# A hybrid attention, scan and latent-attention trunk on one core: five scratch arrays kept by token tile, the scan part projected first, one rotated query projection, and the last softmax denominators on 64 rows

## The chip, the core and the metric

The kernel runs on one core of a Trainium2 chip. A core has five engines that run their own instruction streams side by side: TensorE (PE in the profile; PEld is its weight load), VectorE (DVE), ScalarE (ACT), GpSimd (POOL) and SyncE (SP), which here issues nearly all DMA transfers. TensorE writes to PSUM, eight banks of 128 rows by 512 floats; all other operands lie in SBUF, 128 rows wide; large arrays lie in DRAM and move by DMA on 16 DMA engines. Engines wait for each other by semaphores.

The metric is the time of one execution on the device in microseconds (us), compared as the median of several runs.

## The reference, cut to what matters

Two layers run on 1024 latent tokens and 128 context tokens (T = 1152, nine tiles of 128), width 1024. Layer 0 runs windowed attention (8 heads) beside a bidirectional state-space scan (16 heads of 64, chunks of 128 tokens, both directions); layer 1 is latent attention with 16 heads, whose queries have 64 plain and 32 rotated features:

```python
y = y_f + flip(y_b) + d_skip[:, None] * xs
...
a_out = attn.reshape(b, L, A_WIDTH) * jax.nn.silu(g)
s_out = rms_norm(y.reshape(b, L, SSD_INNER) * jax.nn.silu(z), gnorm_w)
return jnp.concatenate([a_out, s_out], axis=-1) @ w_out
...
xr = jnp.concatenate([rot(x[..., :half]), rot(x[..., half:])], axis=-1)
return x * cos.reshape(shape) + xr * sin.reshape(shape)
...
out = dense_attention(q[:, :, :, None, :], k, v, MLA_SCALE)
return (out.reshape(b, L, MLA_WIDTH) * jax.nn.silu(g)) @ w_out
```

`rot(u)` swaps the two halves of a group of 16 features and negates one. `dense_attention` is a softmax: exponentials of scores, divided by their sum (the denominator). Each layer ends with `x + gate * out`, then comes the next norm. All is float32.

## The kernel before

**Number format.** Most products are done in three matmuls (`mm3`, lines 255 to 258): each operand is split by `split` (245 to 253) into a rounded high part (ScalarE, 249 or 252) and a low part (VectorE, 250 or 253), and high by high, high by low and low by high are summed in one PSUM bank.

**Stages in order.** (1) Modulation and the normalised, transposed input (lines 421 to 456). (2) Keys, values, queries and the gate z of the scan; z goes to `z_d`, feature block by feature block (line 699). (3) `convs` with `attention0` and `chunk_states` woven in (720 to 919): ten blocks of 128 features are projected, convolved, and the eight x blocks written both ways, tokens on rows (`xs_d`, line 900) and features on rows (`xT_d`, 898 and 899). The weights of a block are fetched two blocks ahead by `slab` (line 302). (4) `gates0` (947) multiplies the attention output by its gate and writes `a_d` (959), while `scan_out` starts with two tiles. (5) A loop over the nine token tiles (1158 to 1168): `scan_out` of one tile runs beside `project_out` of the tile before. (6) The latents of layer 1 from `h1_d` (1211 to 1243). (7) `gates1`, the gates of layer 1. (8) Eight pairs of heads (1624 to 1654). (9) The output projection of layer 1, the residual and the last norm, tile by tile (1667 to 1694).

**Scan loop.** `scan_out` loads B and C, `xs_d`, the tile of `xT_d` (990) and `z_d` (993), the states `H_d` and four rows-to-all-partitions copies of the cumulated decays `cum_d` (1004, 512 KB each). It forms the score product `Gp` (984) in a bank of the PSUM ring "pre", the decays with GpSimd (1013) and ScalarE (1015), and the y products (1022). `project_out` loads the attention part (`project_operands`, 1087), and for each half of the output multiplies the attention part (12 matmuls, "plain", PSUM ring "pre") and the scan part (24 matmuls, "scaled", ring "mm"). ScalarE copies plain to SBUF (1105), VectorE adds scaled times a norm factor to it (1106), GpSimd applies gate and residual. A square over the tile (1114) and `norm_T` (1057) follow: transposes, two VectorE operations per half into a buffer of the ring "rt" (two buffers, shared with line 1104), and a write to `h1_d`.

**Pairs.** For each pair `pair_main` does the scores (1470 to 1472), exponentials (ScalarE, 1477), sums (GpSimd, 1506) and values (1491). The operands of the next pair are made in between by `spread`: `quad_weights` and `quad_rope` once in four heads, `operands` (with `rotated`) once a pair, and `head_max`, which finds each query's maximum (1449, VectorE reductions recorded at 209) and sends it to row 96 of the query operand (1441), which the last score product (1472) needs. `quad_rope` does two projections of 128 rotated features per column chunk, one with the weights in order and one with their halves swapped (`swapped`, 1333), and multiplies them by the cosine and sine tables (1367). `gather` divides by the denominators: a one-row product (1522), the row through DRAM (`rd1_d`) to 64 rows and back, a reciprocal on 64 rows, and a copy to all rows (1545). Pair 7 runs its three column chunks in the order 0, 2, 1, and the output projection of tile 0 needs the first of them.

**Order of work.** `Steps` (193) runs deferred parts a given number of score groups later; `pinned` keeps an instruction at its place in the program. For the rest the order of each engine's instructions is set when the program is built, by a planner with its own estimates of durations. Engines then run in that order: an instruction that waits holds all behind it on its engine. Rings of buffers work the same way: a new tile waits for the last reader of the buffer that it takes over.

The scratch arrays touched here, as they were:

```python
a_d = scratch("a_d", [4, 128, T])
xT_d = scratch("xT_d", [KT, 128, T])
z_d = scratch("z_d", [KT, 128, T])
h1_d = scratch("h1_d", [KT, 128, T])
o1_d = scratch("o1_d", [KT, 128, T])
```

A read of one token tile from these takes 512 bytes (128 floats) for each feature and block; a write of a feature block takes long rows. The profile drops digits in the names of DRAM arrays: `h_d` is `h1_d`, `o_d` is `o_d` or `o1_d`, `rd_d` is `rd_d` or `rd1_d`. SBUF tiles lie in four arenas, arenaR, S, G and F.

## Time and profile before

| what | value |
|---|---|
| median of 3 runs | 1848.65 us |
| lowest and highest | 1847.19 and 1849.92 us |
| the profiled execution, its own time | 1851.17 us |
| its span, first to last instruction | 1849.4 us |
| mean granted TensorE clock | 0.952 of full speed |
| DMA | 219.67 MB in 229567 packets, 119 GB/s over the span |
| the hardware queue's share of 16 DMA engines | 39.8% |

How to read the lines further down: a page line gives busy us, share of the span and, behind x, the number of instructions. A line of groups has source line, engine, operation, out<-in, shape and count, then busy us and the mean ns of one, then the engine's idle time before them with what ended it. A waits line names who waited for whom: us in total, times, longest. A timeline line has start, duration, engine, line, operation, and in brackets the idle time just before with what ended it. SPq is SyncE issuing a DMA; its duration is that of the issue, not of the transfer. A line of one source line has count, then min/median/max in ns and the first and last start. Matmuls follow each other closer than their durations, so the pace is read from their starts.

### The profile page before, as it was taken

How to read it: one execution, taken by the hardware profiler on the slowest of the kernel's cores; microseconds unless marked ns; L12 is line 12 of the kernel's file. 1: busy time of each engine (PE TensorE's matmuls, PEld its weight loads, DVE VectorE, ACT ScalarE, POOL GpSimd, SP SyncE). 2: the span in 40 equal slices, each digit the busy share in tenths (PEclk: the TensorE clock that was granted, in tenths of full speed). 3: DMA queues.
4: the chain of work that ended last, by engine and by line, in shares of the span. 5: the costliest groups of instructions: out<-in, count | busy, mean ns of one | idle time of the engine just before them, and what ended most of it. 6: DMA issues, size and time to landing. Idle time of an engine off the chain costs nothing.

```text
span 1849.4 us, 26784 instructions
## 1 busy us (share of the span) xinstructions
PE 1679.6 (91%) x8881; PEld 1293.5 (70%) x8881; DVE 1047.0 (57%) x1977; ACT 866.1 (47%) x1941; POOL 731.0 (40%) x728
## 2 busy tenths in 40 slices
PE   6899998998999778698789999999999999999898
PEld 2799998886876667566569898655665665654486
DVE  3755545556464567678785534665665665565243
ACT  4632222556565456566653422435545634545321
POOL 2510000024333333554634011455665574565432
PEclk8999999999999889899899999999999999999999
DMA  6513323344444889657562533020121121114342
GB/s 224 160 51 113 100 73 110 115 133 137 116 141 140 232 255 279 202 173 222 178 200 86 165 112 101 10 62 23 46 68 32 44 61 45 31 34 122 109 154 91
DMA packets 229567, 219.67 MB, mean 119 GB/s; under 512 B 37283, under 2 KB 194545, under 8 KB 229429
## 3 DMA queue, kind: packets, MB, share of 16 engines
q1 hardware_dynamic: 229284, 217.84, 39.8%
q8 instruction: 70, 1.15, 0.3%
q14 instruction: 69, 0.56, 0.1%
q0 software_dynamic: 144, 0.13, 0.0%
HBM read 156.65 MB, written 56.44 MB: 115 GB/s over the span
## 4 chain that ended last, share of the span: by engine, by line
PE 65%; DMA 13%; ACT 5%; DVE 5%; issue 3%; POOL 2%; SPq 2%; POOLq 0%; DVEq 0%; ACTq 0%
PE acc L256 11%; PE acc L258 10%; PE acc L257 10%; PE acco L1491 6%; PE pp L1449 3%; PE sc L1470 3%; PE sc L1472 3%; PE sc L1471 3%; DMA arenaG<-cum_d 2%; DMA arenaF<-rd_d 2%; DMA rd_d<-arenaF 2%; ACT arenaG L1015 2%; DMA arenaF<-xT_d 1%; PE st L811 1%; DVE arenaR L250 1%
## 5 line engine op out<-in xcount | busy, mean ns | idle before, releaser
L1506 POOL TENSOR_TENSOR arenaG<-arenaG 128x512 f32<-128x512 f32 x256 | 334.2, 1324 | 223.7 <-ACT arenaG L1477 196.6
L256 PE MATMUL acc<-arenaR 128*128 128x384 f32 (+4 forms) x1128 | 392.2, 349 | 31.5 <-ACT arenaR L249 11.7
L257 PE MATMUL acc<-arenaR 128*128 128x384 f32 (+3 forms) x1056 | 362.2, 343 | 0.1
L258 PE MATMUL acc<-arenaR 128*128 128x384 f32 (+4 forms) x1032 | 350.6, 341 | 0.1
L1477 ACT ACTIVATE arenaG<-sc 128x512 f32<-128x512 f32 (+1 forms) x304 | 174.7, 580 | 219.1 <-PE sc L1472 210.8
L256 PEld LDWEIGHTS acc<-arenaR 128*128 128x128 f32 x1128 | 218.2, 194 | 66.4 <-ACT arenaR L249 13.3
L209 DVE TENSOR_REDUCE arenaF<-pp 128x1 f32<-128x384 f32 (+1 forms) x400 | 199.2, 539 | 110.2 <-PE pp L1449 108.7
L257 PEld LDWEIGHTS acc<-arenaR 128*128 128x128 f32 x1056 | 203.9, 193 | 12.6 <-issue 2.8
L258 PEld LDWEIGHTS acc<-arenaR 128*128 128x128 f32 x1032 | 199.1, 193 | 12.7 <-issue 1.5
L250 DVE TENSOR_TENSOR arenaR<-arenaF,arenaR 128x512 fp32r<-128x512 f32 (+2 forms) x144 | 128.4, 904 | 89.9 <-ACT arenaR L249 88.0
L249 ACT CAST arenaR<-arenaF 128x512 fp32r<-128x512 f32 (+3 forms) x160 | 101.0, 648 | 135.0 <-DMA arenaF<-in_ab_w_in_dram 24.2
L1491 PE MATMUL acco<-arenaG 128*64 128x512 f32 (+1 forms) x608 | 150.4, 610 | 0.0
L752 POOL TENSOR_TENSOR arenaG<-arenaS,arenaG 128x512 fp32r<-128x512 f32 x26 | 43.7, 1679 | 155.8 <-PE acco L756 66.7
L1015 ACT ACTIVATE arenaG<-arenaG,arenaF 128x128 f32<-128x128 f32 x288 | 89.8, 390 | 26.6 <-POOL arenaG L1013 26.1
L1449 PE MATMUL pp<-arenaR 96*128 96x384 f32 (+1 forms) x300 | 91.9, 362 | 11.0 <-DVE arenaF L209 10.5
L1470 PE MATMUL sc<-arenaR 96*128 96x512 f32 (+1 forms) x228 | 94.4, 414 | 4.8 <-ACT arenaG L1477 4.5
L1449 PEld LDWEIGHTS pp<-arenaR 96*128 96x128 f32 x300 | 54.7, 190 | 54.2 <-DVE arenaF L209 23.5
L1472 PE MATMUL sc<-arenaR 97*128 97x512 f32 (+1 forms) x228 | 89.0, 394 | 1.3 <-DMA arenaR<-arenaF 1.3
L1471 PE MATMUL sc<-arenaR 96*128 96x512 f32 (+1 forms) x228 | 89.3, 392 | 0.0
L1491 PEld LDWEIGHTS acco<-arenaG 128*64 128x64 f32 x608 | 36.9, 140 | 70.1 <-issue 67.1
L573 POOL TENSOR_TENSOR arenaF<-arenaF 128x256 f32<-128x256 f32 (+1 forms) x27 | 18.4, 684 | 160.1 <-DVE arenaF L571 94.6
L1013 POOL TENSOR_SCALAR_AFFINE_SELECT arenaG<-arenaG 128x512 f32<-128x512 f32 x72 | 61.7, 869 | 50.0 <-ACT arenaF L1009 28.1
(330 smaller groups left out, 3473.6 us busy)
## 6 DMA issues: line engine op xcount, KB each, us to landing
arenaF<-in_ada_w_dram SPq DMA_DIRECT2D x96, 256.0 KB
arenaG<-cum_d SPq DMA_DIRECT2D x36, 512.0 KB
arenaF<-in_ab_w_in_dram SPq DMA_DIRECT2D x51, 256.0 KB
z_d<-arenaF SPq DMA_DIRECT2D x24, 192.0 KB
xs_d<-arenaF SPq DMA_DIRECT2D x8, 576.0 KB
arenaF<-z_d SPq DMA_DIRECT2D x9, 512.0 KB
arenaF<-xT_d SPq DMA_DIRECT2D x9, 512.0 KB
arenaF<-xs_d SPq DMA_DIRECT2D x9, 512.0 KB
```

The costliest lines, as they stand in the source:

```text
L209: f()
L250: lo_eng.tensor_tensor(lo, src, hi.bitcast(F32), ALU.subtract)
L256: pe.matmul(out, ah, bh, start=first, stop=False)
L257: pe.matmul(out, ah, bl, start=False, stop=False)
L258: pe.matmul(out, al, bh, start=False, stop=last)
L1449: pe.matmul(pp[:, 0:w], AQ[s][0:96, t * 128:(t + 1) * 128], AK[s][0:96, k0:k0 + w], start=True, stop=True)
L1470: pe.matmul(sc[:, 0:n], AK[s][0:96, ks], BQ[s][:, qs], start=True, stop=False)
L1471: pe.matmul(sc[:, 0:n], BK[s][:, ks], AQ[s][0:96, qs], start=False, stop=False)
L1472: pe.matmul(sc[:, 0:n], AK[s][:, ks], AQ[s][:, qs], start=False, stop=True)
L1477: act.activation(pf, sc[:, 0:n], AF.Exp, scale=SCALE_M)
L1491: put = lambda: pe.matmul(acc[0][a * 64:(a + 1) * 64], V[:, a], pfs[a], start=(i < 2 and k < 2), stop=(last and k >= len(todo) - 2))
L1506: pool.tensor_tensor(totals[a], first[a] if i == 1 else totals[a], pfs[a], ALU.add)
```

## The change

Five scratch arrays are kept by token tile, so that a tile is read in one piece per partition; the writes of z, xT, a and the attention output go to several tiles at once through `by_tile`. `project_out` multiplies the scan part first, ScalarE scales it while the attention part is multiplied, and VectorE adds. `norm_T` transposes all eight blocks first and writes its result over its input. In layer 1 the 128 rotated features of a quad are ordered so that the two halves of each group lie 64 rows apart; the sine part then comes from the same projection, by two products of 64 rows each with exchanged row halves, and the second projection and `swapped` go. The tables, the split of the weights, and the copies in `operand_set` and `rotated` follow that order, in more and smaller pieces. For pair 7 the denominators are formed on 64 rows by a column block of ones, and divided in place (`gather_last`).

```diff
+    def by_tile(dst, k, t0, src):
+
+        n = src.shape[1] // 128
+        dma.dma_start(dst[t0:t0 + n, :, k].rearrange("t p n -> p t n"), src.rearrange("p (t n) -> p t n", n=128))
...
-    a_d = scratch("a_d", [4, 128, T])
+    a_d = scratch("a_d", [NT, 128, 4, 128])
-    xT_d = scratch("xT_d", [KT, 128, T])
-    z_d = scratch("z_d", [KT, 128, T])
+    xT_d = scratch("xT_d", [NT, 128, KT, 128])
+    z_d = scratch("z_d", [NT, 128, KT, 128])
-    h1_d = scratch("h1_d", [KT, 128, T])
+    h1_d = scratch("h1_d", [NT, 128, KT, 128])
-    o1_d = scratch("o1_d", [KT, 128, T])
+    o1_d = scratch("o1_d", [NT, 128, KT, 128])
...
-                        dma.dma_start(xT_d[fb][:, 0:NL], th[:, 0:NL])
-                        dma.dma_start(xT_d[fb][:, NL:T], th[:, NL + 2:W])
+                        by_tile(xT_d, fb, 0, th[:, 0:NL])
+                        by_tile(xT_d, fb, NLT, th[:, NL + 2:W])
...
-        dma.dma_start(y, xT_d[:, :, tok].rearrange("k p n -> p k n"))
+        dma.dma_start(y, xT_d[c])
...
+        pts = [psum("tr", "pt") for _ in range(2)]
         for q in range(2):
-            pt = psum("tr", "pt")
             for j in range(4):
-                pe.transpose(pt[:, j * 128:(j + 1) * 128], xh[:, (q * 4 + j) * 128:(q * 4 + j + 1) * 128], ident)
-            full = p.tile([128, 4, 128], F32, tag="rt", name="nf", bufs=2)
+                pe.transpose(pts[q][:, j * 128:(j + 1) * 128], xh[:, (q * 4 + j) * 128:(q * 4 + j + 1) * 128], ident)
+        for q in range(2):
+            full = xh[:, q * 512:(q + 1) * 512].rearrange("p (k n) -> p k n", k=4)
...
-            for k in range(4):
-                mm3(plain, at[:, 0, k], at[:, 1, k], *wos[k, q], k == 0, k == 3)
             for k in range(8):
                 mm3(scaled, sT[:, 0, k], sT[:, 1, k], *wos[k + 4, q], k == 0, k == 7)
             tmp = p.tile([128, 512], F32, tag="rt", name="rt", bufs=2)
-            act.copy(tmp, plain)
-            dve.scalar_tensor_tensor(tmp, scaled, r, tmp, ALU.mult, ALU.add)
+            act.activation(tmp, scaled, AF.Identity, scale=r)
+            for k in range(4):
+                mm3(plain, at[:, 0, k], at[:, 1, k], *wos[k, q], k == 0, k == 3)
+            dve.tensor_tensor(tmp, plain, tmp, ALU.add)
...
-        dma.dma_start(AK[i][64:96].bitcast(F32), kp_d[0])
-        dma.dma_start(BK[i][64:96].bitcast(F32), kp_d[1])
-    ones = p7.tile([128, 1], F32, name="ones")
+        for u in range(2):
+            for s in range(2):
+                to, at = slice(64 + s * 16 + u * 8, 72 + s * 16 + u * 8), slice(u * 16 + s * 8, u * 16 + s * 8 + 8)
+                dma.dma_start(AK[i][to].bitcast(F32), kp_d[0, at])
+                dma.dma_start(BK[i][to].bitcast(F32), kp_d[1, at])
+    ones = p7.tile([128, 64], F32, name="ones")
...
-            for a, b, w, at in ((0, 64, 64, 0), (64, 96, 32, 256)):
-                o = slice(at, at + 4 * w)
...
+            split(qh[:, k, 0:256].rearrange("p (h d) -> p h d", h=4), ql[:, k, 0:256].rearrange("p (h d) -> p h d", h=4), raws[k][:, :, 0:64], scale)
             for s in range(2):
-                dve.tensor_copy(dst[:, :, :, s], src[:, :, :, 1 - s].bitcast(F32))
+                for u in range(2):
...
+                    split(part(qh), part(ql), raws[k][:, :, at:at + 8], scale)
...
-            for i, t in enumerate(ts):
-                after(1, dve.tensor_tensor, t, uq_proj(qh, ql, 256 + 128 * i, cols), tab[:, i], ALU.mult)
-                yield
+            acc = uq_proj(qh, ql, 256, cols)
+            after(1, dve.tensor_tensor, ts[0], acc, tab[:, 0], ALU.mult)
+            for s in range(2):
+                at, to = slice(s * 64, (s + 1) * 64), slice((1 - s) * 64, (2 - s) * 64)
+                after(1, dve.tensor_tensor, ts[1][to], acc[at], tab[at, 1], ALU.mult)
+            yield
...
+            i, h = (4 * Q + 2 * pr + a) % NSET, 2 * pr + a
+            for s in range(2):
+                to, r = slice(64 + s * 16, 80 + s * 16), slice(s * 64 + h * 16, s * 64 + h * 16 + 16)
+                for dst, src in ((AQ, quads[Q][1][0]), (BQ, quads[Q][1][1])):
+                    dma.dma_start(dst[i][to].bitcast(F32), src[r].bitcast(F32))
...
+    def gather_last(j, op, q0, n, totals):
+
+        qs = slice(q0, q0 + n)
+        gt = p7.tile([128, n], F32, tag=f"gt{n}", name="gt1")
+        rb = p7.tile([128, n], F32, tag=f"rb{n}", name="rb1")
+        dma.dma_start(gt, g1_d[j, :, qs])
+
+        def sums():
+            den = spare("den")
+            for a in range(2):
+                pe.matmul(den[a * 64:(a + 1) * 64, 0:n], ones, totals[a], start=True, stop=True)
+            dve.tensor_tensor(gt, op[:, qs], gt, ALU.mult)
+            after(1, divided, den)
+
+        def divided(den):
+            dve.reciprocal(rb, den[:, 0:n])
+            dve.tensor_tensor(gt, gt, rb, ALU.mult)
+            by_tile(o1_d, j, q0 // 128, gt)
+        steps.behind(1, sums)
...
+        if j == 7:
+            return gather_last(j, op, q0, n, totals)
...
-            make, n_make = [operands(pair + 1)], 22
+            make, n_make = [operands(pair + 1)], 19
```

The other reads and writes of the five arrays (`z_d`, `a_d`, `h1_d`, `o1_d`) change as those of `xT_d` do.

More of the change, by code (lines that the diff above doesn't have):

```diff
@@ L958, in gates0 @@
             dve.tensor_tensor(th, th, ot, ALU.mult)
-            dma.dma_start(a_d[b, :, cols], th)
+            by_tile(a_d, b, c * 3, th)
             if b == 3:
@@ L1521, in sums @@
             for a in range(2):
-                pe.matmul(den[a * 64:a * 64 + 1, 0:n], ones, totals[a], start=True, stop=True)
+                pe.matmul(den[a * 64:a * 64 + 1, 0:n], ones[:, 0:1], totals[a], start=True, stop=True)
             after(1, store, den)
```

37 lines of the change are left out of this document (16 added, 21 removed).

## The prediction

> **What bounds the kernel now.** I read the page first, then busy time by stage, then the waits of TensorE and the timelines around the longest ones.
>
> ```profile
> span 1849.4 us, 26784 instructions
> PE 1679.6 (91%) x8881; PEld 1293.5 (70%) x8881; DVE 1047.0 (57%) x1977; ACT 866.1 (47%) x1941; POOL 731.0 (40%) x728
> ```
>
> TensorE (PE) is busy 91% of the span; 169.8 us are left. The stage view (stretch, its length, busy us per engine, granted clock, DMA share, GB/s) says where they lie. Rows in order: convolutions with attention; attention gates; the loop of scan and output projection; the latent layer's gates; the eight head pairs.
>
> ```profile
> 318.00:640.00 322.00, 294.18 (x1590) 233.93 (x1590) 179.68 (x288) 187.83 (x380) 98.81 (x103) 0.94 0.49 141
> 640.00:741.00 101.00, 81.27 (x466) 68.99 (x465) 67.20 (x103) 56.15 (x128) 38.90 (x39) 0.89 0.94 270
> 741.00:969.00 228.00, 184.72 (x1070) 144.22 (x1070) 173.29 (x200) 138.60 (x342) 118.21 (x118) 0.90 0.65 194
> 1005.00:1150.00 145.00, 142.15 (x822) 133.73 (x821) 60.62 (x137) 49.86 (x121) 18.26 (x30) 1.00 0.41 119
> 1150.00:1736.00 586.00, 553.02 (x2454) 336.92 (x2454) 337.18 (x695) 286.32 (x621) 349.83 (x273) 0.97 0.18 51
> ```
>
> Two kinds of stage. In the gates and the pairs TensorE is busy 98% and 94% of the time (142.15 of 145, 553.02 of 586), no other engine over 60%: a matmul taken out there is time taken out. In the scan loop TensorE lacks 43.3 us (228 - 184.72) and VectorE is busy 76%; there waits decide. The longest:
>
> ```profile
> PE Gp L984 <- ACT arenaF L1105: 26.2, 4, 13.2
> ```
>
> ```profile
> 768.78 0.59 ACT L1105 COPY arenaF<-acca 128x512 f32<-128x512 f32 x1 [5.89 <-DMA h_d<-arenaF]
> ```
>
> Four times, 26.2 us in all, the score product Gp of a later tile waits for a PSUM bank that ScalarE's copy at L1105 must empty. In the worst (13.2 us) ScalarE itself stood idle 5.89 us, until a write into h1_d had left the buffer that the copy needs: the ring "rt" of two, shared by L1104 and L1063.
>
> **Part by part.**
>
> *norm_T in place.* The h1_d writes now leave from xn, so L1104 no longer shares "rt" with them. Of the 13.2 us wait the 5.89 go; what was late before them (ScalarE's exponentials and a square, until 762.9) stays. The new wait is the next tile's square into xn, which has one buffer; it comes a tile later (228 us for nine tiles, 25 each) and the late write was over by 768.78, so I cost it at nothing, and at 5.9 a tile if that cover were gone. **-5.9**.
>
> *Reading xT_d, z_d, a_d, h1_d in rows of 4 KB or 2 KB instead of 512-byte pieces.* First bandwidth, in two stretches of 4 us when the queue was full, the first with 512-byte pieces of z_d, the second with 4 KB rows:
>
> ```profile
> DMA packets 2086, 1.06 MB, mean 266 GB/s; under 512 B 38, under 2 KB 2082, under 8 KB 2086
> ...
> q1 hardware_dynamic: 2086, 1.06, 91.5%
> ```
>
> ```profile
> DMA packets 327, 1.22 MB, mean 304 GB/s; under 512 B 30, under 2 KB 30, under 8 KB 327
> ...
> q1 hardware_dynamic: 327, 1.22, 99.7%
> ```
>
> 266/0.915 = 291 GB/s against 304/0.997 = 305 at full share: 5%, or 0.1 us on a transfer of 512 KB. The Trainium skill ("DMA: Bandwidth & Descriptors", Specifications) names 512 B as the smallest transfer for line rate; by it this edit would give nothing, and the sum would be 7.5 us smaller. On bandwidth the two stretches nearly agree with it. What the pieces do cost stands on SyncE:
>
> ```profile
> 870.25 0.37 SPq L993 DMA_DIRECT2D arenaF<-z_d  x1
> 870.72 4.50 SPq L1004 DMA_DIRECT2D arenaG<-cum_d  x1
> ```
>
> An issue takes 0.37 us, but the one behind xT_d and z_d (1024 pieces each, 2 x 512 KB / 512 B) takes 4.50. In the chain of work that ended last (start, us, what) this transfer, and two reads of xT_d, stand at full length:
>
> ```profile
> 838.80 8.30 DMA arenaF<-xT_d
> ```
>
> ```profile
> 870.72 9.45 DMA arenaG<-cum_d
> ```
>
> ```profile
> 898.67 10.37 DMA arenaF<-xT_d
> ```
>
> ```profile
> 807.35 5.97 DMA arenaG<-cum_d
> ```
>
> The last is the same 512 KB in 4 KB rows without the hold-up: 5.97. I take 4.1 for the held issue (4.50 - 0.37), and for the two reads half of their excess (8.30 + 10.37 - 2 x 5.97 = 6.7, so 3.4), since part of it is other traffic. **-7.5**, bounds 0 and -10.8. In the other stages I cost the reads at nothing: 640 to 741 runs the DMA at a share of 0.94 either way, and the output loop feeds a busy TensorE.
>
> *Writing in 512-byte pieces.* z_d, a_d and o1_d are written 384 or 512 pieces at a time over long stages; xT_d goes from 256 to 1152 pieces a block, eight times, right after a write of the same kind:
>
> ```profile
> L900 SPq DMA_DIRECT2D xs_d<-arenaF x8: 370/383/546, 391.0 to 637.9; - x8
> ```
>
> xs_d is 1152 pieces (9 tiles x 128 rows) and issues in 0.38 us. Two in a row are what held 870.72 up for 4.1 us: bounds 0 and 8 x 4.1 = 33 us of SyncE. Hidden, it lies under the weights being fetched two blocks ahead, a block being some 32 us (322 / 10): I take 0.
>
> *Scan part first in project_out.* The same 72 matmuls; now ScalarE scales while the 12 plain ones run, and VectorE's addition empties the bank that Gp waits for. Instructions and engines stay even (one ScalarE, one VectorE operation for one of each). ScalarE gets a lead of 12 x 0.23 us = 2.7 (the spacing of these matmuls at full pace, rows 1740.78 and 1741.01 below), but VectorE now stands behind it: 0, bounds +-2.7 for each of the other three waits.
>
> *One rotated projection.* uq_proj is 6 matmuls of 384 columns; one of two goes, for 3 column chunks and 4 quads: 72.
>
> ```profile
> 1256.37 0.34 PE L256 MATMUL acc<-arenaR 128*128 128x384 f32 x1
> 1256.54 0.33 PE L257 MATMUL acc<-arenaR 128*128 128x384 f32 x1
> 1256.71 0.34 PE L258 MATMUL acc<-arenaR,arenaS 128*128 128x384 f32 x1
> 1256.89 0.34 PE L256 MATMUL acc<-arenaR 128*128 128x384 f32 x1
> ```
>
> They overlap, so the spacing counts: 0.52/3 = 0.173 us, and 72 x 0.173 = **-12.5** (54 in the pairs, 18 in the gates). What is added:
>
> ```profile
> L250 DVE TENSOR_TENSOR arenaR<-acc,arenaR 64x384 fp32r<-64x384 f32 x36 | 19.8, 551 | 11.5 <-ACT arenaR L249 10.7
> ```
>
> ```profile
> L253 DVE SCALAR_TENSOR_TENSOR arenaS<-arenaF,vecs,arenaR 128x128 fp32r<-128x128 f32 x6 | 2.3, 379 | 5.9 <-ACT arenaR L252 5.9
> ```
>
> ```profile
> L1333 DVE CAST arenaR<-arenaR x8: 209/216/220, 1075.7 to 1383.9; 128x128 fp32r<-128x128 f32 x8
> L1333 DVE CAST arenaS<-arenaS x8: 208/216/219, 1075.9 to 1384.7; 128x128 fp32r<-128x128 f32 x8
> ```
>
> ```profile
> L1236 DVE TENSOR_TENSOR arenaF<-acc,arenaF x8: 178/180/181, 987.2 to 1023.0; 128x32 f32<-128x32 f32 x8
> ```
>
> VectorE: 12 more half-height products at 0.55 (+6.6), 8 splits of 128 columns become 32 of 32 columns at about 0.18 (+2.7), 16 swaps at 0.216 go (-3.5): +5.8 us, over stages where it is idle 42% or more of the time. ScalarE gains 24 small splits, 4.3 us at the same 0.18. Both lie beside matmuls; uncovered they would cost at most 5.8. SyncE:
>
> ```profile
> L1404 SPq DMA_DIRECT2D arenaR<-arenaF x24: 512/552/870, 1112.5 to 1596.9; - x24
> ```
>
> rotated issues 8 instead of 4 per pair: +32 x 0.55 = 17.6 us; operand_set +24, by this row 13 at most. Queued behind them is the row of maxima (L1441) that a score product needs; rotated goes out at a pair's start, the maxima some ten steps later. If all were exposed it would be 4 x 0.55 = 2.2 us in each of 7 pairs, 15.4. Of VectorE and SyncE together I let 1.5 us through, as both have long idle stretches there (DMA share 0.18). Net **-11.0**, bounds -12.5 and +8.7 (5.8 and 15.4 in full).
>
> *Last denominators.* Pair 7 no longer sends its sums through DRAM. Now (the chain, then TensorE):
>
> ```profile
> 1709.02 3.83 DMA rd_d<-arenaF
> ```
>
> ```profile
> 1730.75 4.70 DMA arenaF<-o_d
> ```
>
> ```profile
> 1736.56 0.79 PE L256 MATMUL acc<-arenaR 128*128 128x512 f32 x1 [6.63 <-ACT arenaR L249]
> 1737.15 0.63 PE L257 MATMUL acc<-arenaR 128*128 128x512 f32 x1
> 1737.58 0.63 PE L256 MATMUL acc<-arenaR 128*128 128x512 f32 x1
> ```
>
> ```profile
> 1740.78 0.39 PE L257 MATMUL acc<-arenaR 128*128 128x512 f32 x1
> 1741.01 0.40 PE L258 MATMUL acc<-arenaR 128*128 128x512 f32 x1
> ```
>
> From the sums (stored at 1709.0) to the first operand's load (1730.75) are 21.7 us; then TensorE has stood 6.63 us, and starts at half pace: 0.43 us apart against 0.23; over the 3.4 us to about 1740 that loses 3.4 x 0.20/0.43 = 1.6. The new path is a reciprocal and a product:
>
> ```profile
> L511 DVE RECIPROCAL arenaS<-arenaS x1: 1953/1953/1953, 110.5 to 110.5; 128x288 f32<-128x288 f32 x1
> ```
>
> 1953/288 = 6.8 ns a column, 3.5 us for 512 as an estimate, plus 0.7 for the product (0.55 for 384 columns, L250 above). The load can then start near 1709 + 4 + 4 (a write like the one at 1709.02) = 1717, 14 us earlier, and TensorE goes from the last scores straight into the output: -6.6 - 1.6 = **-8.2**. What is late next is the residual input, needed 24 matmuls (5.5 us) later. Bounds -8.2 and 0.
>
> **Sum.** -5.9 - 7.5 - 11.0 - 8.2 = -32.6. The profiled execution took 1851.17 us (span 1849.4 and 1.8 around it): 1818.6. The median of the three runs, 1848.65, lies 2.5 lower, so I forecast 1816 (-1.8%).
>
> **The rivals.** (1) *The scan loop gains nothing.* For it: VectorE at 76%, bandwidth alike in both forms, and all instructions are put in order anew at build time, so that waits can come back elsewhere. Against it: ScalarE's 5.89 and SyncE's 4.50 have named causes that the diff removes. Left are -11.0 - 8.2: 1851.2 - 19.2 - 2.5 = 1829.5. The rule of the Trainium skill quoted above ("DMA: Bandwidth & Descriptors", Specifications) speaks for this rival. (2) *The loop's waits all fall together.* Idle 43.3 us, and a granted clock of 0.90: if two thirds of the idle go (-29 instead of -13.4), 1851.2 - 29 - 19.2 - 2.5 = 1800.5. (3) *SyncE is held up in the convolutions*, on the other side: xT_d's 1152 pieces behind xs_d's 1152 hold the next weights by 4.1 us in 8 blocks, and TensorE waits each time: +33. With rival 1's loop that is 1829.5 + 33 = 1862.5, with my own 1849. It decides only where weights arrive less than 4 us early; TensorE's 294 of 322 us leave 28 idle, so some such place exists, eight do not. (4) *The pairs give nothing back*: the matmuls go, but ScalarE's exponentials or VectorE's maxima set the pace, -11.0 becomes -2: 1825. Against it: neither is over 60% busy there.
>
> **How the numbers follow.** Forecast 0.55, rivals 0.20, 0.13, 0.06, 0.06. Measurement of this kernel tells about 0.2% (3.7 us) from no change; only rival 3, and the far end of rivals 1 and 4, get to 1845 or above: faster 0.90, same 0.04, slower 0.06. From 1798 (just past rival 2) to 1841 (rival 1 with the pairs giving nothing, 1829.5 + 11) leaves out rival 3 and the ends of the others, some two in ten.
>
> **What would show it.** Right: no wait of the first evacuation in project_out on a write of h1_d; cum_d issues all under 1 us; 72 fewer matmuls of 384 columns and a stretch of pairs some 11 us shorter; no gap of 6.63 us before the first output product. Wrong: SyncE issues of 3 us or more between 360 and 640, a score product waiting for maxima rows by more than the present few us, or a scan loop still near 228 us.

## The result and the profile after

The changed kernel took 1840.59 us in the median of 20 runs (1831.03 to 1850.28), the kernel before 1851.78 in 20 runs on the same chip (1844.57 to 1859.22). The ratio is 0.9935, with a 95% interval of 0.9915 to 0.9955: 12 us faster, with 8 to 16 possible. Forecast were 33. The profiled execution of the changed kernel took 1847.63 us, near the slow end of its runs.

The page after (span; busy time by engine), and the stage view over the stretches that answer to those of before, each shifted to where its stage now lies. Columns: stretch, length, busy us of PE, PEld, DVE, ACT, POOL with counts, granted clock, DMA share, GB/s.

```profile
span 1845.5 us, 26718 instructions
...
PE 1692.1 (92%) x8809; PEld 1291.7 (70%) x8809; DVE 1062.7 (58%) x1998; ACT 868.6 (47%) x1959; POOL 729.8 (40%) x727
```

```profile
640.00:741.00 101.00, 83.33 (x473) 69.32 (x473) 67.61 (x105) 55.54 (x129) 37.70 (x37) 0.89 0.88 268
741.00:960.00 219.00, 188.49 (x1084) 146.89 (x1085) 176.04 (x203) 143.02 (x346) 122.71 (x121) 0.94 0.61 205
995.00:1135.00 140.00, 138.08 (x796) 129.10 (x794) 60.88 (x139) 51.07 (x131) 18.87 (x30) 1.00 0.42 118
1135.00:1736.00 601.00, 568.00 (x2407) 340.96 (x2408) 349.15 (x714) 287.58 (x629) 344.69 (x272) 0.93 0.20 52
```

72 matmuls have gone (8881 to 8809), yet TensorE is busy 12.5 us longer: 1692.1 against 1679.6. The last row says where: the pairs now run at a granted clock of 0.93, not 0.97, and take longer, not shorter. (The row ends at 1736 us in both kernels; some 5 us of it are output products now, which begin at 1731.02 and not at 1736.56.) The rest of the change can be read off three places. The wait on h1_d's write is gone from the list of TensorE's waits (741 to 960 us); other, shorter ones have come up in its place:

```profile
PE accs L258 <- ACT arenaS L251: 7.5, 3, 3.4
PE Gp L991 <- DVE arenaF L1114: 7.1, 3, 4.2
PE acca L258 <- DVE arenaG L1114: 2.7, 1, 2.7
```

SyncE's issues of cum_d, before and then after (duration in ns: least, median, longest; first and last start):

```profile
L1004 SPq DMA_DIRECT2D arenaG<-cum_d x36: 320/392/4495, 621.7 to 930.3; - x36
```

```profile
L1011 SPq DMA_DIRECT2D arenaG<-cum_d x36: 319/325/873, 624.1 to 919.6; - x36
```

The longest fell from 4.50 to 0.87 us. And the gap of 6.63 us ahead of the output product has gone: TensorE comes straight from the value products (the timeline of after; start, us, engine, line, operation).

```profile
1729.15 1.94 PE L1502 MATMUL acco<-arenaG 128*64 128x512 f32 x8
1731.02 0.50 PE L258 MATMUL acc<-arenaR 128*128 128x512 f32 x1
1731.36 0.39 PE L259 MATMUL acc<-arenaR 128*128 128x512 f32 x1
```

So by stage: the writes of x1_d, one for each token tile of the scan loop, ended at 975.4 us before and end at 965.6 now, 9.8 us earlier; the last write of g1_d, the end of the gates, is 13.6 us earlier (1148.5 to 1134.9). But the last maxima product of the pairs starts at 1675.9, against 1676.4. **The pairs gave the lead back, 13 us of it, though 54 of the 72 lost matmuls were theirs.** This execution had a clock of 0.943, its kernel 0.948 in the mean of the 20 runs, so it shows the loss larger than it is in the median. The experiments look for what took it.

### The profile page after: what moved, and what is told of

It is laid out like the page before. It is cut to its first block, busy times and chain, and to the rows that moved or that the text cites. A ratio compares the mean times of both kernels' runs of the same rounds, so it can differ in the third digit from the quotient of the medians.

```text
span 1845.5 us, 26718 instructions
## 1 busy us (share of the span) xinstructions
PE 1692.1 (92%) x8809; PEld 1291.7 (70%) x8809; DVE 1062.7 (58%) x1998; ACT 868.6 (47%) x1959; POOL 729.8 (40%) x727
## 4 chain that ended last, share of the span: by engine, by line
PE 65%; DMA 14%; DVE 7%; ACT 4%; POOL 3%; issue 3%; SPq 3%; POOLq 0%; DVEq 0%; ACTq 0%
PE acc L258 11%; PE acc L260 10%; PE acc L259 10%; PE acco L1502 5%; PE sc L1481 3%; PE sc L1483 3%; PE pp L1460 3%; PE sc L1482 3%; DMA arenaF<-rd_d 2%; DMA arenaG<-cum_d 1%; DVE arenaF L211 1%; DMA arenaF<-in_ada_w_dram 1%; DVE arenaR L252 1%; ACT arenaG L1022 1%; DMA arenaF<-in_ab_w_in_dram 1%
## 5 line engine op out<-in xcount | busy, mean ns | idle before, releaser
L258 PE MATMUL acc<-arenaR 128*128 128x384 f32 (+4 forms) x1104 | 382.7, 347 | 17.8 <-ACT arenaR L251 5.3
L259 PE MATMUL acc<-arenaR 128*128 128x384 f32 (+3 forms) x1032 | 353.2, 342 | 0.1
L260 PE MATMUL acc<-arenaR 128*128 128x384 f32 (+4 forms) x1032 | 350.4, 341 | 0.1
L258 PEld LDWEIGHTS acc<-arenaR 128*128 128x128 f32 x1104 | 213.5, 194 | 52.8 <-issue 13.5
L260 PEld LDWEIGHTS acc<-arenaR 128*128 128x128 f32 x1032 | 198.9, 193 | 12.4 <-issue 2.5
L259 PEld LDWEIGHTS acc<-arenaR 128*128 128x128 f32 x1032 | 199.2, 193 | 10.7 <-issue 1.1
L1502 PE MATMUL acco<-arenaG 128*64 128x512 f32 (+1 forms) x608 | 155.0, 627 | 0.0
L1460 PE MATMUL pp<-arenaR 96*128 96x384 f32 (+1 forms) x300 | 96.9, 380 | 15.5 <-DVE arenaF L211 14.8
```

Source lines behind the costliest of these rows:

```text
L258: pe.matmul(out, ah, bh, start=first, stop=False)
L259: pe.matmul(out, ah, bl, start=False, stop=False)
L260: pe.matmul(out, al, bh, start=False, stop=last)
L1460: pe.matmul(pp[:, 0:w], AQ[s][0:96, t * 128:(t + 1) * 128], AK[s][0:96, k0:k0 + w], start=True, stop=True)
L1502: put = lambda: pe.matmul(acc[0][a * 64:(a + 1) * 64], V[:, a], pfs[a], start=(i < 2 and k < 2), stop=(last and k >= len(todo) - 2))
```

## The experiments

Times of one kernel spread over some 15 us, so each kernel was run against before on its own chip, and the table gives ratios. The us are the ratio's distance from 1 times 1850. The clock is the mean over the runs of the granted clock; before had 0.952 over 35 runs.

| kernel | ratio (95% interval) | us | clock |
|---|---|---|---|
| the change | 0.9935 (0.9915 to 0.9955) | -12.0 | 0.948 |
| layout_only | 0.9964 (0.9947 to 0.9981) | -6.7 | 0.953 |
| norm_order_only | 0.9988 (0.9972 to 1.0004) | -2.2 | 0.954 |
| scan_parts | 0.9973 (0.9956 to 0.9990) | -5.0 | 0.954 |
| rotated_only | 0.9982 (0.9965 to 1.0000) | -3.3 | 0.948 |
| last_den_only | 0.9970 (0.9947 to 0.9994) | -5.5 | 0.952 |
| no_rot | 0.9937 (0.9913 to 0.9961) | -11.7 | 0.954 |
| lean | 0.9948 (0.9930 to 0.9966) | -9.6 | 0.950 |
| filler | 1.0057 (1.0036 to 1.0077) | +10.5 | 0.949 |
| few_issues | 0.9910 (0.9875 to 0.9946) | -16.7 | 0.950 |
| whole_product | 0.9853 (0.9820 to 0.9885) | -27.2 | 0.953 |
| whole_splits | 0.9893 (0.9856 to 0.9929) | -19.8 | 0.950 |
| late_division | 0.9914 (0.9886 to 0.9943) | -15.9 | 0.950 |
| after_22 | 0.9899 (0.9868 to 0.9929) | -18.7 | 0.950 |
| after_22_again | 0.9876 (0.9833 to 0.9919) | -22.9 | 0.953 |
| before_25 | 1.0002 (0.9979 to 1.0025) | +0.4 | 0.951 |
| swap_scalar | 0.9886 (0.9862 to 0.9911) | -21.1 | 0.952 |
| swap_scalar_22 | 0.9822 (0.9794 to 0.9851) | -32.9 | 0.957 |
| swap_scalar_25 | 0.9867 (0.9839 to 0.9894) | -24.6 | 0.953 |

### The parts alone

Four kernels hold one part of the diff each, applied to before. First the arrays:

```diff
-    xT_d = scratch("xT_d", [KT, 128, T])
-    z_d = scratch("z_d", [KT, 128, T])
+    xT_d = scratch("xT_d", [NT, 128, KT, 128])
+    z_d = scratch("z_d", [NT, 128, KT, 128])
...
-        dma.dma_start(zs, z_d[:, :, tok].rearrange("k p n -> p k n"))
+        dma.dma_start(zs, z_d[c])
```

> Only the five arrays kept by token tile; order of project_out, norm_T, the rotated projections and the last denominators as before. Theory 1 (what the change gained before the pairs is real and stays, and the pairs alone give back): the scan loop shortens by some 4 to 8 us, SyncE's issue of cum_d behind xT_d and z_d falls from 4.50 to below 1 us, and the total is 4 to 8 us under before. Rival (the loop gained by norm_T in place and the new order alone, the layout gives nothing): within 2 us of before. A second rival (SyncE held in the convolutions by 512-byte pieces): the last convolution product comes 2 us or more later and the total is not below before.

It took 6.7 us off, as theory 1 had it. The longest issue of cum_d shows why:

```profile
L1009 SPq DMA_DIRECT2D arenaG<-cum_d x36: 319/371/937, 622.0 to 917.6; - x36
```

Before, seven issues between 300 and 1000 us took over 2 us; here, and in the changed kernel, none does. That also answers the rival of a SyncE held in the convolutions: in the changed kernel's answer for xT_d the longest of the writes there takes 1.27 us (least, median, longest; ns), and the first write of x1_d starts at 751.6 us in both kernels.

```profile
L300 SPq DMA_DIRECT2D xT_d<-arenaF x16: 365/571/1273, 367.5 to 614.9; - x16
```

Then norm_T and the order in project_out, alone:

```diff
...
-            for k in range(4):
-                mm3(plain, at[:, 0, k], at[:, 1, k], *wos[k, q], k == 0, k == 3)
             for k in range(8):
                 mm3(scaled, sT[:, 0, k], sT[:, 1, k], *wos[k + 4, q], k == 0, k == 7)
...
-            act.copy(tmp, plain)
-            dve.scalar_tensor_tensor(tmp, scaled, r, tmp, ALU.mult, ALU.add)
+            act.activation(tmp, scaled, AF.Identity, scale=r)
+            for k in range(4):
+                mm3(plain, at[:, 0, k], at[:, 1, k], *wos[k, q], k == 0, k == 3)
+            dve.tensor_tensor(tmp, plain, tmp, ALU.add)
```

> Only norm_T in place and the scan part first in project_out; arrays as before. Forecast of this part was -5.9. Theory 1: -2 to -6, all of it between 741 and 969 us. Rival (the layout carries the loop's gain): within 2 us of before. In both the wait of ScalarE for h1_d's write ahead of project_out's first evacuation is gone.

2.2 us by the ratio, and its interval holds zero: the runs alone don't tell theory 1 from the rival. So the two were put together.

> The five arrays by token tile together with norm_T in place and the scan part first; rotated projections and last denominators as before. Alone they gave 0.9964 and 0.9988. If the two take away the same waits of the scan loop: 0.996 to 0.998, no more than the arrays alone, TensorE idle 32 to 35 us between 741 and 975 (45 before, 34 with the arrays alone, 33 with the order alone). If they add up, as the forecast had it (-13.4): 0.993 to 0.995, and 30 us idle or less.

Together they gave 5.0 us, not more than the arrays alone. The stage view from the first to the last write of x1_d shows it, for before, layout_only, norm_order_only and scan_parts:

```profile
751.60:975.40 223.80, 180.59 (x1034) 141.80 (x1033) 165.93 (x195) 133.61 (x324) 115.68 (x116) 0.89 0.65 195
```

```profile
747.30:961.60 214.30, 180.27 (x1043) 142.21 (x1043) 167.26 (x195) 133.93 (x325) 116.94 (x116) 0.90 0.64 203
```

```profile
748.80:965.70 216.90, 186.95 (x1076) 146.31 (x1075) 170.13 (x196) 136.92 (x334) 118.92 (x118) 0.93 0.65 198
```

```profile
746.20:962.70 216.50, 187.18 (x1063) 146.66 (x1062) 171.01 (x196) 137.05 (x334) 119.29 (x120) 0.91 0.62 198
```

Length less PE's busy time is what TensorE lacks: 43.2, 34.0, 30.0 and 29.3 us. The figures are rough: one profile each, and the stretches hold 1034 to 1076 recorded matmuls. Each part alone takes away 9 to 13 of it, both 14. **They largely remove the same waits.** The four waits of Gp for ScalarE's copy, 26.2 us before, are still 20.1 us in layout_only; in the other two they are gone, and three shorter ones for VectorE's addition (8.2 and 6.8 us) stand in their place. Once norm_T worked in place, little was left for the arrays to take away. The times alone do not prove it: 5.0 us may be 1.9 to 8.1, and the two parts sum to 8.9.

The last denominators alone:

```diff
+            for a in range(2):
+                pe.matmul(den[a * 64:(a + 1) * 64, 0:n], ones, totals[a], start=True, stop=True)
...
+            dve.reciprocal(rb, den[:, 0:n])
+            dve.tensor_tensor(gt, gt, rb, ALU.mult)
```

> Only the last pair's denominators on 64 rows in the chip's memory. Forecast of this part was -8.2. Theory 1: the 6.63 us gap ahead of the output product goes, but half-clock spells in the last pair take part of it back: -2 to -5, and the stretches before the last pair stay as before. Rival (the tail's full gain is there, and the loss in the changed kernel's tail came with the other parts): -7 to -8.

5.5 us (1.1 to 9.8): between the two theories. All profiles together say more. From the start of the last maxima product to the end of the span, the eight profiled kernels without this part lie between 173.0 and 176.5 us (mean 174.3), the twelve with it between 161.6 and 169.6 (mean 166.1): 8.2 us. These kernels differ in more than this part; the profile of the part alone has 167.2 against 173.0 before.

And the one rotated projection:

```diff
...
-            for i, t in enumerate(ts):
-                after(1, dve.tensor_tensor, t, uq_proj(qh, ql, 256 + 128 * i, cols), tab[:, i], ALU.mult)
-                yield
+            acc = uq_proj(qh, ql, 256, cols)
+            after(1, dve.tensor_tensor, ts[0], acc, tab[:, 0], ALU.mult)
+            for s in range(2):
+                at, to = slice(s * 64, (s + 1) * 64), slice((1 - s) * 64, (2 - s) * 64)
+                after(1, dve.tensor_tensor, ts[1][to], acc[at], tab[at, 1], ALU.mult)
+            yield
...
```

> Only the one rotated projection (72 matmuls fewer, with its extra VectorE products, small splits and SyncE issues, and the pace of 19). Forecast of this part was -11.0. Theory 1 (the matmuls' time is given back in the pairs as half-clock spells): the latent gates gain about 3 us, the seven stretches between the pairs gain nothing or lose up to 10, with more than 31 us at half clock between 1150 and 1655, and the total is between -3 and +7 us of before. Rival (the matmuls' gain is real, what was lost in the pairs came from another part or from a chance new order): -8 to -11.

3.3 us, not 8 to 11: the rival falls, the loss belongs to this part. Its clock fell with it, 0.952 to 0.948. In the clock records of all 20 profiles the granted clock is either 1.0 or 0.5, so a run spends 2 x span x (1 - clock) at half clock: 192 us against 177. Over the 35 runs of before one us more at half clock goes with 0.44 us more time. That is a correlation; by its slope those 15 us stand for some 6, as an estimate. And without this part the change is as fast as with it:

> The change without the one rotated projection (tables, weights and pace of the pairs as before). By the sum of the three parts run alone (-6.6 by medians, -2.2, -5.5) 1836; by forecast (-21.6) 1829. Theory 1 (only the rotated projection brings the half clock): half clock 172 to 178 and 1836 or less, so no slower than the whole change. Rival (the parts take from each other wherever they stand together, and any new order brings half clock): 1840 or more, half clock 185 or more.

0.9937: the clock stayed up (0.954), as theory 1 said. Its 1836 us would be a ratio of 0.992, which lies inside the interval (0.9913 to 0.9961), and so does 0.994, the rival's 1840; whether the other parts too bring less together than apart is not settled by this.

### Fewer matmuls, or the work that replaces them?

lean is before, with the second product taken from the first projection (the rotary part is then another than the reference's): 72 matmuls fewer and nothing added, at the pace of 19 (see below).

```diff
+            acc = uq_proj(qh, ql, 256, cols)
             for i, t in enumerate(ts):
-                after(1, dve.tensor_tensor, t, uq_proj(qh, ql, 256 + 128 * i, cols), tab[:, i], ALU.mult)
-                yield
+                after(1, dve.tensor_tensor, t, acc, tab[:, i], ALU.mult)
+            yield
...
-            make, n_make = [operands(pair + 1)], 22
+            make, n_make = [operands(pair + 1)], 19
```

> Before, with one of the two rotated projections left out and nothing added: both products are taken from the first one (the rotary output is then another than the reference's); no half-height products, no small splits, no more SyncE issues. 72 matmuls fewer, 12.5 us of TensorE by my row. Time at half clock in a run is reckoned as 2 x span x (1 - mean granted clock): before 177 us over 35 runs, rotated_only 192. Theory 1a (the added VectorE and SyncE work makes the waits and so the half clock): about -10 to -12, half clock as before, 172 to 182. Theory 1b (fewer matmuls alone leave TensorE with more pauses, so the clock falls): -2 to -6, half clock 187 to 197.

filler is the converse: everything that the rotated projection adds, and the second projection computed and thrown away.

```diff
...
                 after(1, dve.tensor_tensor, ts[1][to], acc[at], tab[at, 1], ALU.mult)
             yield
+            uq_proj(qh, ql, 256, cols)
+            yield
```

> The one rotated projection with all that it adds on VectorE, ScalarE and SyncE, but the second projection is still computed and thrown away, and the pace is 22 as before: the matmuls of before with the added work. Theory 1a (the added work costs): +3 to +8 against before, half clock 187 or more. Theory 1b (only the missing matmuls cost): within 2 us of before, half clock 172 to 182.

Theory 1a, twice: the matmuls alone are worth 9.6 us, and the work that replaces them costs 10.5, more than I had given even this theory. lean's clock of 0.950, 183 us at half clock, is just outside what theory 1a had. Three rows of the changed kernel's groups show what that work is on VectorE (busy us, mean ns of one); the middle one is the first rotary product, for comparison:

```profile
L211 DVE TENSOR_TENSOR arenaF<-acc,arenaF 64x384 f32<-64x384 f32 x24 | 13.3, 555 | 0.5
L211 DVE TENSOR_TENSOR arenaF<-acc,arenaF 128x384 f32<-128x384 f32 x12 | 6.7, 558 | 14.8 <-PE acc L260 9.9 <-DMA arenaF<-in_k_rope1t_dram 2.1 <-issue 1.5
L255 DVE SCALAR_TENSOR_TENSOR arenaS<-arenaF,vecs,arenaR 128x32 fp32r<-128x32 f32 x32 | 9.8, 349 | 6.1 <-ACT arenaR L254 6.0
```

A product of 64 rows takes as long as one of 128 (555 and 558 ns).

### Where it is lost: the fourth pair

The stage view of the fourth pair, from its first score product to the next pair's: before, lean, changed kernel.

```profile
1384.10:1454.10 70.00, 67.22 (x308) 40.94 (x306) 41.77 (x89) 35.07 (x79) 41.57 (x32) 0.98 0.14 37
```

```profile
1376.21:1443.81 67.60, 65.67 (x308) 40.52 (x308) 41.55 (x90) 34.99 (x79) 41.91 (x32) 1.00 0.15 40
```

```profile
1371.80:1450.91 79.11, 73.52 (x312) 43.65 (x311) 45.89 (x99) 36.15 (x84) 42.38 (x33) 0.91 0.16 38
```

Nine us in one pair, with the clock at 0.91. VectorE's timeline at its start, in the changed kernel:

```profile
1363.71 1.69 DVE L211 TENSOR_TENSOR arenaF<-acc,arenaF 128x384 f32<-128x384 f32 x3 [3.31 <-PE acc L260]
1365.44 2.42 DVE L211 TENSOR_REDUCE arenaF<-pp 128x1 f32<-128x384 f32 x5
1369.62 3.00 DVE L255 SCALAR_TENSOR_TENSOR arenaS<-arenaF,vecs,arenaR 128x32 fp32r<-128x32 f32 x4 [1.77 <-ACT arenaR L254]
...
1375.75 4.92 DVE L211 TENSOR_REDUCE arenaF<-pp 128x1 f32<-128x384 f32 x11
...
1380.78 0.27 DVE L1440 TENSOR_SCALAR arenaF<-arenaF 128x4 fp32r<-128x4 f32 x2
```

The three products of the last chunk, then four small splits, and behind them a string of maxima without a pause. The pair's last maxima are done (1380.78 + 0.27) 9.2 us after its first score product. Before (first row below) that was 6.4 us (1390.31 + 0.27, from 1384.14); in whole_product (second row), which has one rotary product fewer to a chunk, 6.5 (1375.23 + 0.27, from 1368.96):

```profile
1390.31 0.27 DVE L1429 TENSOR_SCALAR arenaF<-arenaF 128x4 fp32r<-128x4 f32 x2
```

```profile
1375.23 0.27 DVE L1438 TENSOR_SCALAR arenaF<-arenaF 128x4 fp32r<-128x4 f32 x2
```

What follows on TensorE, in the timeline and the stage view of the changed kernel:

```profile
1381.07 1.22 PE L1483 MATMUL sc<-arenaS,arenaR 97*128 97x512 f32 x2 [1.61 <-DMA arenaS<-arenaF]
```

```profile
1410.61 1.15 PE L1460 MATMUL pp<-arenaR 96*128 96x384 f32 x2 [3.00 <-DVE arenaF L211]
```

```profile
1372.00:1379.00 7.00, 6.10 (x25) 3.39 (x24) 7.00 (x17) 2.10 (x5) 1.70 (x2) 1.00 0.53 103
1380.00:1386.00 6.00, 4.93 (x12) 1.99 (x13) 2.38 (x12) 2.92 (x10) 1.27 (x1) 0.50 0.34 89
1387.00:1410.00 23.00, 20.61 (x97) 13.20 (x95) 14.02 (x24) 12.53 (x26) 16.09 (x12) 1.00 0.11 28
1411.00:1417.00 6.00, 6.00 (x15) 3.23 (x16) 2.59 (x8) 1.19 (x2) 2.55 (x2) 0.50 0.24 65
```

VectorE is busy 7.00 of 7 us; a score product waits 1.61 us for its row of maxima, and the clock stands at 0.50 in the whole window after it. Thirty us later TensorE waits 3.00 us for maxima, and again 0.50. Before, TensorE had both waits too:

```profile
1391.09 0.69 PE L1472 MATMUL sc<-arenaS,arenaR 97*128 97x512 f32 x2 [1.63 <-DMA arenaS<-arenaF]
1412.71 0.44 PE L1449 MATMUL pp<-arenaR 96*128 96x384 f32 x1 [1.08 <-DVE arenaF L209]
```

The first was as long as now. The second has grown by 1.9 us; in it VectorE, in the changed kernel, itself waits for denominators:

```profile
1408.20 1.90 DVE L1303 TENSOR_TENSOR arenaF<-arenaF 128x128 f32<-128x128 f32 x2 [1.65 <-DMA arenaF<-rd_d]
```

By the stage view TensorE's idle time in the pair grows from 2.8 to 5.6 us, and its busy time from 67.2 to 73.5. So of the nine us some three are waits and six are slower matmuls: by the clock records the pair has 13.7 us at half clock, and had 3.4.

Three changed kernels cut one candidate each, and a fourth the wait at 1410. First SyncE's issues:

```diff
-            i, h = (4 * Q + 2 * pr + a) % NSET, 2 * pr + a
-            for s in range(2):
-                to, r = slice(64 + s * 16, 80 + s * 16), slice(s * 64 + h * 16, s * 64 + h * 16 + 16)
-                for dst, src in ((AQ, quads[Q][1][0]), (BQ, quads[Q][1][1])):
-                    dma.dma_start(dst[i][to].bitcast(F32), src[r].bitcast(F32))
+            i, r = (4 * Q + 2 * pr + a) % NSET, slice((2 * pr + a) * 32, (2 * pr + a + 1) * 32)
+            for dst, src in ((AQ, quads[Q][1][0]), (BQ, quads[Q][1][1])):
+                dma.dma_start(dst[i][64:96].bitcast(F32), src[r].bitcast(F32))
```

> The changed kernel with rotated issuing 4 transfers of 32 rows a pair, as before, in place of 8 of 16 rows (the rows of the rotary part then stand in another order than the reference needs): 28 issues of about 0.58 us fewer in the pairs, 16 us of SyncE; all else as changed (1841 us over 20 runs, half clock 193). Theory S (SyncE's longer queue at a pair's start sends the rows of maxima and the denominators late, and TensorE waits and drops to half clock): 1829 to 1835, the wait of 1.6 us for the maxima's rows at the start of the fourth pair below 1.0, that pair 75 us or less in place of 79. Theories V and D (below): within 3 us of 1841.

Then the two half-height products made one:

```diff
-            for s in range(2):
-                at, to = slice(s * 64, (s + 1) * 64), slice((1 - s) * 64, (2 - s) * 64)
-                after(1, dve.tensor_tensor, ts[1][to], acc[at], tab[at, 1], ALU.mult)
+            after(1, dve.tensor_tensor, ts[1], acc, tab[:, 1], ALU.mult)
```

> The changed kernel with the second rotary product as one VectorE operation of 128 rows, not swapped, in place of two of 64 rows (another rotary result than the reference's): 12 VectorE operations of 0.55 us fewer. Theory V (VectorE's added operations hold the maxima): 1831 to 1837 here or in the next run, whole_splits. Theories S and D: within 3 us of 1841.

Then the small splits:

```diff
-            for s in range(2):
-                for u in range(2):
-                    at = 64 + u * 16 + s * 8
-                    part = lambda w: w[:, k, 256 + s * 64:320 + s * 64].rearrange("p (h u f) -> p h u f", h=4, u=2)[:, :, u]
-                    split(part(qh), part(ql), raws[k][:, :, at:at + 8], scale)
+            split(qh[:, k, 256:384].rearrange("p (h d) -> p h d", h=4), ql[:, k, 256:384].rearrange("p (h d) -> p h d", h=4), raws[k][:, :, 64:96], scale)
```

> The changed kernel with the rotary columns of the weights split in one piece of 128 columns, not in four of 32 (columns in another order than the reference needs): 24 VectorE and 24 ScalarE operations fewer. Theory V: 1831 to 1837 here or in whole_product. Theories S and D: within 3 us of 1841.

And the division of the pair before:

```diff
-            after(2, pinned, dve.tensor_tensor, gt, gt, rb, ALU.mult)
-            after(3, gated, gt)
+            after(5, pinned, dve.tensor_tensor, gt, gt, rb, ALU.mult)
+            after(6, gated, gt)
```

> The changed kernel with the two VectorE products of a pair's division put three steps later (5 and 6 in place of 2 and 3 steps behind the reading back of the denominators), nothing else. Theory D (VectorE, which works in order, stands at a product whose denominators have not come back from DRAM, and the maxima behind it hold TensorE's banks, so a wait of 3 us and 6.8 us of half clock follow): the waits of VectorE for rd_d in the pairs, 18.9 us in the changed kernel's profile, fall below 8, the 3.0 us wait of TensorE in the fourth pair is gone, 1830 to 1837. If the maxima wait for another reason: within 3 us of 1841.

**Theory V (VectorE) is borne out.** Twelve VectorE products of 0.55 us fewer, 6.7 us of VectorE, bring the ratio from 0.9935 to 0.9853, 15 us; the intervals don't touch. The fourth pair then takes 67.85 us at full clock:

```profile
1368.96:1436.81 67.85, 65.67 (x310) 40.71 (x308) 42.92 (x92) 35.06 (x79) 41.88 (x32) 1.00 0.17 40
```

All 20 profiles agree with it. From its first exponential to that of the next pair, the fourth pair takes 73.5 to 79.8 us in the eight kernels that have the half-height products, and 66.3 to 72.3 in the twelve that have not.

Two things limit this. Every copy of the changed kernel that keeps the one projection came out below 0.9935, whatever was altered in it, and the planner's order is new in each, so part of the 15 us may be what any new order brings; against few_issues and late_division they are 10 to 11. And how the products lengthen the second wait is not shown: in it VectorE stands for denominators, which is theory D's wait, yet in whole_product TensorE waits 1.08 us there, as before.

The small splits count for some 8 us (0.9893), with intervals that still overlap. Fewer issues (0.9910) and the later division (0.9914) can't be told from the changed kernel; the division put later didn't do what it was to do, VectorE stood 20.5 us for rd_d in the pairs instead of below 8. Theories S and D are not shown; they are not excluded at the size of 4 us.

### The pace

The pace is the number of items, steps in making the next pair's operands, that `spread` asks for over the 36 steps of a pair: the larger it is, the earlier each item comes.

```diff
-            make, n_make = [operands(pair + 1)], 19
+            make, n_make = [operands(pair + 1)], 22
```

> The changed kernel with the pace of 22 in place of 19: the making of the next pair's operands is asked for a little earlier. If the pace carries the half clock in the pairs: half clock falls from 193 toward 177 and the time by 4 us or more against the changed kernel (1841), to about 1836. If not: within 2 us of 1841.

> The changed kernel at pace 22 once more, on another chip and beside the two others. If its 0.9899 was no accident of its six runs: 0.987 to 0.992. If it was: 0.993 or more.

Both times it is faster than the change: 0.9899 and 0.9876. The third pair shows how. In the changed kernel the timelines of VectorE and of TensorE read

```profile
1331.83 0.29 DVE L1303 TENSOR_TENSOR arenaF<-arenaF 128x128 f32<-128x128 f32 x1 [3.43 <-DMA arenaF<-rd_d]
```

```profile
1332.65 0.69 PE L1460 MATMUL pp<-arenaR 96*128 96x384 f32 x1 [3.34 <-DVE arenaF L211]
1333.13 0.63 PE L1481 MATMUL sc<-arenaR 96*128 96x512 f32 x1
```

and in after_22

```profile
1332.31 0.51 DVE L1303 TENSOR_TENSOR arenaF<-arenaF 128x128 f32<-128x128 f32 x1 [3.70 <-DMA arenaF<-rd_d]
```

```profile
1330.15 1.94 PE L1502 MATMUL acco<-arenaG 128*64 128x512 f32 x8
1333.35 0.44 PE L1460 MATMUL pp<-arenaR 96*128 96x384 f32 x1 [1.26 <-DVE arenaF L211]
```

VectorE stands as long for the denominators (3.43 and 3.70 us, with the maxima behind it), but at 22 the order of the products differs: eight value products lie in the stand, TensorE waits 1.26 instead of 3.34, and keeps its clock (0.44 for the next product, not 0.69). The pair takes 69.4 us instead of 74.8. So it is in all profiles: the third pair, counted as the fourth above, takes 73.1 to 75.2 us in the eight kernels with one projection and the pace of 19, and 69.4 to 72.5 in the four with 22 or 25. lean is one of the eight (74.7), so the pace of 19 costs some 4 us here without any of the added work. Is that the change's, or would any version gain?

> The kernel before with the pace of 25 in place of 22, so that, as with 22 in the changed kernel, the next pair's operands are asked for three items earlier than its own list of steps needs; nothing else. If an earlier pace helps any version of this kernel: 0.993 to 0.997 of before. If 19 was too low only for the changed kernel, whose list holds more VectorE work behind each item: 0.998 to 1.005.

Nothing (1.0002): with the list of before, asking earlier does not help.

### A version that keeps the gain

The swap is needed, but not on VectorE. swap_scalar multiplies in one operation and lets ScalarE put the halves in each other's rows.

```diff
-            for s in range(2):
-                at, to = slice(s * 64, (s + 1) * 64), slice((1 - s) * 64, (2 - s) * 64)
-                after(1, dve.tensor_tensor, ts[1][to], acc[at], tab[at, 1], ALU.mult)
+            after(1, dve.tensor_tensor, ts[1], acc, tab[:, 1], ALU.mult)
             yield
-            after(2, pool.tensor_tensor, ts[0], ts[0], ts[1], ALU.add)
-            after(3, act.copy, rh[:, cols], ts[0])
...
+            swapped = rl[:, cols].bitcast(F32)
+            for s in range(2):
+                after(2, act.copy, swapped[(1 - s) * 64:(2 - s) * 64], ts[1][s * 64:(s + 1) * 64])
+            after(3, pool.tensor_tensor, ts[0], ts[0], swapped, ALU.add)
+            after(4, act.copy, rh[:, cols], ts[0])
...
```

> The changed kernel at pace 19, with the second rotary product as one VectorE operation of 128 rows; ScalarE then copies its two halves to each other's rows (24 ScalarE copies of 64 rows more), and GpSimd's sum comes a step later. The result is the reference's. Theory V (the 12 added VectorE operations at the quad changes hold the maxima behind them): the changed kernel's ratio to before, 0.9935, falls toward that of whole_product, 0.9853; I expect 0.985 to 0.989. Rival (any work added to this chain, on whichever engine, delays the operands that rotated sends): 0.992 or more.

> The same with the pace of 22. If pace and half-height products are two cures of one congestion of VectorE at the quad changes: no better than the better of the two alone, 0.985 to 0.990. If they are separate: 0.982 or less.

> swap_scalar with the pace of 25. If the earlier the better: below 0.982 (swap_scalar_22 had 0.9822). If 22 is about where the operands are early enough and VectorE's maxima are pushed back beyond it: 0.983 to 0.988.

0.9886 at the pace of 19: the same work on another engine costs 9 us less, and the rival's 0.992 lies outside the interval; so it is VectorE, not the length of the chain. With 22 it is 0.9822, 1818.43 us in the median, **33 us faster than before (28 to 38) and, by the two ratios, 21 faster than the change**; 0.9822 lies just above what I gave two separate cures (0.982 or less). With 25 it is 0.9867: not the earlier the better. Its profile (page; fourth pair):

```profile
span 1814.7 us, 26742 instructions
...
PE 1670.9 (92%) x8809; PEld 1284.0 (71%) x8809; DVE 1058.5 (58%) x1986; ACT 879.3 (48%) x1983; POOL 733.6 (40%) x727
```

```profile
1368.35:1437.71 69.36, 67.09 (x307) 40.89 (x307) 42.23 (x90) 34.89 (x79) 41.57 (x32) 0.98 0.17 36
```

TensorE is now busy 21 us less than in the changed kernel for the same 8809 matmuls.

## Why the prediction failed, step by step

- **One rotated projection (-11.0): wrong, and the main error.** The 72 matmuls are worth what I said (lean: -9.6, with 6.3 to 13.0 possible; forecast -12.5). What failed is the sentence that lets 1.5 us through "as both have long idle stretches there". Idle time over 586 us says nothing of the 15 us in which the added work falls: it comes when a quad is made, where VectorE also owes the maxima, and there it was busy 7.00 of 7 us. Measured, the added work costs 10.5 us (filler), and the loss is larger than the waits, because the clock halves behind them: in the fourth pair one wait grew from 1.08 to 3.00 us, the time at half clock from 3.4 to 13.7. My price for the 32 small splits was off too: 0.18 us each, measured 0.35. Rival 4 named the mechanism, that VectorE's maxima set the pace, and I put it aside with the same average, "neither is over 60% busy there", and a chance of 0.06; yet its -2 for this part is near the -3.3 measured (0 to 6.5), and in the changed kernel's profile the pairs came out longer than before. In the sum I priced waits at their length only, and left the pace of 19 uncosted, some 4 us in the third pair.
- **Reading in 4 KB and 2 KB rows (-7.5): right**, -6.7 (3.5 to 9.8), by the step I named: no issue of SyncE is held any longer. Its two terms, the held issue and the reads' excess, were not told apart.
- **norm_T in place (-5.9): right in mechanism, wrong in the sum.** The wait of 13.2 us is gone, but it and the held issue cover the same lack of TensorE; together they are no -13.4 but -5.0 (scan_parts; 1.9 to 8.1). The last write of x1_d agrees: at 972.8 us in the mean of six profiles without both parts, at 966.2 in twelve with them.
- **Scan part first (0): not told apart.** It was run only with norm_T in place.
- **Writing in 512-byte pieces (0): right**; no write of xT_d issues for over 1.27 us, and the loop starts where it did.
- **Last denominators (-8.2): right.** The gap of 6.63 us has gone. The part is worth 5.5 us by the times of the part alone (1.1 to 9.8), 5.8 by its profile and 8.2 over all profiles; the changed kernel's own profile shows 3.4. That one of these equals the forecast is luck.
- The rival "the loop gains nothing" is excluded by layout_only; "SyncE held in the convolutions" by the row of xT_d's writes.

What stays open: the single parts sum to 17.7 us (6.7 + 2.2 + 3.3 + 5.5) and the change gives 12; with intervals of 3 to 4 us either way on each part, that difference is not clear of noise. By the slope above, half clock explains some 7 us of the forecast's missing 21; how the rest divides between overlap in the loop and the planner's order, which differs in every one of these kernels, was not separated.

## What to carry to other kernels

Work taken from TensorE and given to an engine with 40% idle time is paid where it falls: look at that engine in the ten us around it, and at who is queued behind it. A wait of TensorE must be priced with the half clock behind it, and two causes of one wait count once. A half-height operation costs a whole one; here ScalarE swapped the halves at less cost to the whole.

## What the hardware showed

- The granted clock had two values and a fixed step. In the clock records of all 20 profiles it is 1.0 or 0.5, and the 539 spells at half clock, without the last of each run, lasted 3.4, 6.8, 10.2, 13.7 or 17.1 us.
- Short waits were enough to drop the clock. Counted in all 20 profiles from 1150 us on, for waits of TensorE that began at full clock: half clock began between their start and 4 us after their end in 9 of 62 waits of 0.7 to 0.9 us, in 16 of 32 of 1.1 to 1.3, in 23 of 24 of 1.7 to 2.0 and in all 72 above 2.0. The Trainium skill ("TensorE: Matmul & The Clock Gate", Why this matters for your kernels) warns of gaps above about 3 us; here waits of 1.7 us nearly always did it, and the wait of 1.26 us in after_22 is one of those that did not.
- A small VectorE operation stands while GpSimd adds. In the changed kernel, with VectorE in the first fence and GpSimd in the second:

```profile
1222.66 1.24 DVE L255 SCALAR_TENSOR_TENSOR arenaS<-arenaF,vecs,arenaR 128x32 fp32r<-128x32 f32 x1
1223.82 0.55 DVE L211 TENSOR_REDUCE arenaF<-pp 128x1 f32<-128x384 f32 x1
1224.29 0.24 DVE L255 SCALAR_TENSOR_TENSOR arenaS<-arenaF,vecs,arenaR 128x32 fp32r<-128x32 f32 x1
```

```profile
1222.57 1.28 POOL L1517 TENSOR_TENSOR arenaG<-arenaG 128x512 f32<-128x512 f32 x1 [3.81 <-ACT arenaG L1488]
```

  The same split takes 0.24 us alone and 1.24 beside GpSimd's sum, ending with it; twice more (1.31 each) in the 3.00 us at 1369.62. The Trainium skill ("SBUF — State Buffer", SBUF: two separate sides) has the two share a port pair that one holds for a whole instruction, against VectorE operations with two SBUF inputs; the trace agrees, and the maxima, which read PSUM, keep their 0.55 (98 of them lie wholly beside such a sum).
